# Down-phase operands requested in the last up unit, norm squares summed in PSUM, low parts on GpSimd, three more buffers

## The chip, the cores and the metric

The kernel runs on one core of a Trainium2 chip. The core has TensorE (matrix products into PSUM), VectorE (DVE in the profile), ScalarE (ACT), GpSimd (POOL) and SyncE (SP), which issues nearly all DMA transfers here. Every engine has a queue of its own that it works off in order, and engines wait for each other by semaphores. The metric is the device time in microseconds (us) of one execution.

## What is computed

One layer of a decoder trunk for a prompt of 2048 tokens and a sample group of 8 times 4 tokens, 2080 tokens in all, with 1024 channels, in 32-bit floating point. Attention in a window of 128 and a state-space block run side by side, are normalised, and go through an output projection; then comes a gated feed-forward network (FFN) with a short convolution:

```python
merged = jnp.concatenate([_rmsnorm(attn, p['g_attn']), _rmsnorm(ssm, p['g_ssm'])], axis=-1)
x = x + merged @ p['w_out']
f, conv_new = _conv_ffn(_rmsnorm(x, p['norm_ffn']), conv_prev,
                        p['w_up'], p['conv_w'], p['conv_b'], p['w_down'])
x = x + f

def _conv_ffn(h, prev, w_up, conv_w, conv_b, w_down):
    L = h.shape[1]
    up = h @ w_up
    buf = jnp.concatenate([prev.astype(up.dtype), up], axis=1)
    c = conv_b + sum(conv_w[i] * buf[:, i:i + L] for i in range(CONV_W))
    a, g = jnp.split(c, 2, axis=-1)
    return (jax.nn.silu(g) * a) @ w_down, buf[:, -(CONV_W - 1):]
```

with `_rmsnorm(x, g)` = x · rsqrt(mean(x²) + 1e-5) · g, and one more such norm at the very end.

## The kernel before

**Precision.** Every matrix product is made of three. An operand is split into a high part (a rounding to fp32r) and a low part (the rest); `mm3` adds high·high, high·low and low·high in one PSUM bank. `split` makes the two parts: line 83 casts the high part, usually on ScalarE, and line 84 subtracts it for the low part, on VectorE or GpSimd as its last argument says.

**Channels lie on the 128 partitions, tokens in the free dimension.** The work comes in stages: projections, attention and state space, then the output projection, then the FFN in two groups of tokens (`gi` 0 and 1), each with an up phase and a down phase.

**Output projection.** `TILES3` are eight tiles of 260 tokens, loop variable `it`. For each, eight output blocks `m` are computed (eight times three matmuls each, tiles `wo`), in a ring of four PSUM banks. The input block `xm` is loaded (line 1171), the product is added (line 1176) and the sum is stored to `x2scr` (line 1177). `xm` has twelve buffers. At the end of a tile `sumsq` forms the sum of squares of the eight blocks: ScalarE squares a block, VectorE adds it to `ss` in SBUF (line 133). The norm itself is computed inside the next tile, after block 1: `ffn_norm` calls `rstd_psum`, which sums over partitions with a matmul against ones (line 115), takes logarithm and exponential on ScalarE and one Newton step on VectorE (lines 119 to 121), all in the PSUM bank; eight VectorE instructions (line 1143) then scale the blocks, and each is stored to `h2scr` (line 1144). The pool `pst` has two banks for this. The last tile's norm is computed in `finish_front`, within the first up unit; only behind it are the pool of `xm` and `pst` closed, whose places go to the pool `hb` (operand q0) and to the two banks `psv` of the up phase.

**The up phase** has 21 units `j` for each `gi`. A unit uses Winograd-like sums so that seven products replace eight; the operands x0, t2, q1 and q0, each as high and low parts, are made once per phase. For `gi` 0 they come from sums stored during the output projection: `begin_ffn` loads and splits t2, `load_q(1)` q1, and `load_q(0)`, called from `finish_front`, q0. `load_wup` prepares a unit's weights (on GpSimd the low parts and four sums, lines 1265 to 1269). A unit takes eight tiles from the ring `c2`, which has ten buffers (`CB`): two `ca`, two `cb`, two `cc0`, two `cc1`. The results, high and low part, leave from the `cc` tiles to `actscr` (line 1331). `unit` takes two hooks: `begin` runs after its second product, `mid` between the two halves of its fourth.

**The down phase** runs over token tiles (two of 512 for `gi` 0; 448, 352 and 256 for `gi` 1), each with 21 operand blocks `i` and eight output blocks `m`, that is 24 matmuls for an operand block (tiles `dn`). `load_a` loads the block's high and low part (`ah`, `al`) from `actscr` into two `c2` buffers, for up to three blocks ahead (line 1464); `load_wd` loads and splits the weights (`wdr`, line 1437). In the first tile the output blocks 2, 3, 6 and 7 of the first two operand blocks are put off until the third (`ULATE` = 2), because their banks are those that the last up unit used last: blocks 0 to 3 use the pool of `ux`, 4 and 5 that of `u` (tag u2), 6 and 7 `psv`.

Instructions are put in order at build time: each engine's queue is filled by priority (the order of the code, moved forward where `tc.high_priority` says so) among what is ready, and tiles get their buffers then.

Of the kernel before, what the change touches and what calls it, by code (L numbers as in the profile page):

```python
# [18 lines left out]
P = 128  # L19
# [43 lines left out]
HPD = 90  # L63
# [46 lines left out]

def rstd_psum(c, pool, ps, ss, n, ones, nm):

    nc = c.nc
    ps = ps[:, :n]
    nc.tensor.matmul(ps, ones, ss, start=True, stop=True)
    r0 = pool.tile([P, n], F32, tag="r0", name=f"r0_{nm}")
    nc.scalar.activation(r0, ps, AF.Ln, bias=c.eps)
    nc.scalar.activation(r0, r0, AF.Exp, scale=-0.5)
    nc.vector.scalar_tensor_tensor(ps, ps, EPS, r0, ALU.add, ALU.mult)
    nc.vector.scalar_tensor_tensor(ps, ps, -0.5, r0, ALU.mult, ALU.mult)  # L120
    nc.vector.scalar_tensor_tensor(ps, ps, 1.5, r0, ALU.add, ALU.mult)
    return ps


def sumsq(c, pool, xs, n, nm, eng=None):

    nc = c.nc
    ss = pool.tile([P, n], F32, tag="ss", name=f"ss_{nm}", bufs=2)
    nc.scalar.activation(ss, xs[0], AF.Square)
    for k, x in enumerate(xs[1:]):  # L130
        sq = pool.tile([P, n], F32, tag="sq", name=f"sq_{nm}_{k}", bufs=3)
        nc.scalar.activation(sq, x, AF.Square)
        (eng or nc.vector).tensor_tensor(ss, ss, sq, ALU.add)
    return ss

# [503 lines left out]
def body(tc, a):  # L639
# [16 lines left out]
    with ExitStack() as top:  # L656
# [473 lines left out]
        with after_preload():  # L1130
# [7 lines left out]
            def ffn_norm(it, xs, ss):  # L1138
                t0, n = TILES3[it]
                r = rstd_psum(c, p3b, pst.tile([P, 512], F32, tag="st", name=f"st_f_{it}"), ss, n, ones[1024], f"f_{it}")  # L1140
                for k in range(KD):
                    h = xs[k]
                    nc.vector.scalar_tensor_tensor(h, xs[k], g_ffn[:, k : k + 1], r, ALU.mult, ALU.mult)
                    nc.sync.dma_start(h2scr[:, k, t0 : t0 + n], h)

            def begin_ffn():

                p3m_close()
                stg_close()
                st.p3e_close()  # L1150
                ffn.sp, ffn.sp_close = pool("fsp", "right")
                ffn.up, ffn.up_close = pool("fup", "right", 2)
                ffn.c2, ffn.c2_close = pool("fc2", "right", CB)
                ffn.hc, ffn.hc_close = pool("fhc", "right")
                for sub in range(2):
                    t2 = ffn.t2[sub] = hi_lo(ffn.hc, [4, W], f"t2{sub}", 0)
                    for k in range(0, 4, 2):
                        s = ffn.c2.tile([P, 2, W], F32, tag="c2", name=f"t2r_{sub}_{k}")
                        nc.sync.dma_start(s, t2scr[:, sub, k : k + 2])
                        split(nc, *[t[:, k : k + 2] for t in t2], s, nc.scalar, nc.vector)  # L1160

            old = None
            for it, (t0, n) in enumerate(TILES3):
# [5 lines left out]
                for m in range(KD):  # L1169
                    xm = p3b.tile([P, n], F32, tag="xm", name=f"xm_{it}_{m}", bufs=12)  # L1170
                    nc.sync.dma_start(xm, xTv[:, m, t0 : t0 + n])
# [17 lines left out]
                if it == len(TILES3) - 2:  # L1189
                    begin_ffn()  # L1190
                old = (it, xs, sumsq(c, p3b, xs, n, f"f_{it}", nc.vector))
        ps_close()
# [85 lines left out]
        def load_q(i):  # L1278
            for sub in range(2):
                q = (ffn.q0, ffn.q1)[i][sub] = hi_lo((hb, hd)[i], [2, 4, W], f"q{i}{sub}", 0)  # L1280
                for k in range(4):
                    s = c2.tile([P, 2, W], F32, tag="c2", name=f"q{i}r_{sub}_{k}")
                    nc.sync.dma_start(s, qscr[:, sub, i, k])
                    with tc.high_priority(offset=HPD):
                        split(nc, *[t[:, :, k] for t in q], s, nc.scalar, nc.vector if i else (nc.gpsimd, nc.vector)[k % 2])

# [145 lines left out]
        def load_wd(gi, j, t0):  # L1432
# [17 lines left out]
            return w  # L1450

        def down(gi, beside):

            old = None
            for ti, (t0, n) in enumerate(TILESD[gi]):
# [4 lines left out]

                def load_a(j):
                    hl = [dt([P, n], F32R, f"a{i}_{t0}_{j}") for i in "hl"]
                    for i, t in enumerate(hl):
                        ffn.last_sp = nc.sync.dma_start(t.bitcast(F32), actscr[:, j, 1 - i, t0 : t0 + n]).ins
                    return hl

                def one(i, m):
# [4 lines left out]

                hls = {}
                for i, j in enumerate(order):
                    for ahead in range(i, min(i + 3, NF)):
                        if ahead not in hls:
                            hls[ahead] = load_a(order[ahead])
                    ahl[i] = hls[i], load_wd(gi, j, t0)
# [28 lines left out]
        def prepare(gi):  # L1507
# [3 lines left out]
            for f in (load_sums, load_last):  # L1511
                for sub in range(2):
                    yield from f(gi, sub)

        def last_norm():
            next(last, None)

        for gi in range(2):
            for j in range(NF):
                if (gi, j) != (0, 0):  # L1520
                    ws = load_wup(gi, j)
                unit(gi, j, ws, None if j or gi else finish_front, last_norm if gi and j == 0 else None)
            beside = prepare(1) if gi == 0 else iter(())
# [128 lines left out]
```

## Time and profile before

| what | us |
|---|---|
| device time, median of 3 runs | 2220.59 |
| lowest and highest of these | 2218.52, 2222.08 |
| the profiled execution | 2218.95 |
| its span, first to last instruction | 2217.2 |
| TensorE busy in the span | 2055.2 (93%) |
| VectorE, ScalarE, GpSimd busy | 1323.1, 1054.1, 1200.4 |
| last wo matmul to first up matmul | 765.68 to 771.17 |
| first up phase's end to the first down matmul | 1217.25 to 1227.38 |
| second up phase's end to the first down matmul | 1927.09 to 1943.62 |

The profile is one execution. A row of its timeline gives the start (us from the span's start), the duration, the engine, the line of the kernel, the operation, the tiles written and read, their shape and how many instructions are merged in the row; behind it in brackets stands the idle time of that engine just before, with the instruction that ended it. SPq is SyncE's queue, where DMA transfers are issued. A wait view sums such idle time by who waited for whom. A window view gives each engine's busy time in a stretch, the clock granted to TensorE (1.00 is full) and the share of the DMA engines.

### The profile page before, as it was taken

To read this page: it belongs to the slowest core of one execution; us is meant where nothing else is said; L and a number is where in the kernel's file an instruction comes from. 1 tells how busy PE (TensorE), PEld (TensorE's weight loads), DVE (VectorE), ACT (ScalarE), POOL (GpSimd) and SP (SyncE) were. 2 spreads that over 40 slices of the span, in tenths; PEclk is the share of its full clock that TensorE was granted. 3 is DMA by queue.
4 is the path that set the end of the run, shared out by engine and by line. 5 is a ranking of instruction groups with operands and counts; after the bars stand their busy time and mean duration, and the time that the engine had idled before them with its cause. 6 is when DMAs were issued, how large, how long until landed. Compare 5 with 4: busy or idle time off the path is not lost.

```text
span 2217.2 us, 41459 instructions
## 1 busy us (share of the span) xinstructions
PE 2055.2 (93%) x14685; PEld 1926.3 (87%) x14685; DVE 1323.1 (60%) x3310; ACT 1054.1 (48%) x2459; POOL 1200.4 (54%) x1184
## 2 busy tenths in 40 slices
PE   8969999978998889999999898999999999799997
PEld 8957878857998889999999686789999999788997
DVE  8859898358566766766666165227766666601231
ACT  6525564675443356666666233225655665602111
POOL 4857776334455466666665453446666666822211
PEclk9979999989999999999999899999999999999999
DMA  7865434686478733333333795834323333573643
GB/s 230 255 149 157 123 107 130 128 232 189 147 236 255 236 125 117 108 96 110 108 107 102 248 284 177 292 130 152 112 93 110 106 101 102 175 191 118 206 131 98
DMA packets 294352, 347.59 MB, mean 157 GB/s; under 512 B 42344, under 2 KB 250864, under 8 KB 294128
## 3 DMA queue, kind: packets, MB, share of 16 engines
q1 hardware_dynamic: 294144, 344.94, 51.5%
q8 instruction: 116, 1.90, 0.4%
q14 instruction: 92, 0.75, 0.1%
HBM read 232.70 MB, written 107.80 MB: 154 GB/s over the span
## 4 chain that ended last, share of the span: by engine, by line
PE 70%; DVE 10%; DMA 7%; POOL 4%; issue 4%; ACT 3%; SPq 2%; DVEq 0%; POOLq 0%; ACTq 0%
PE ux L1345 20%; PE u L1345 16%; PE dn L90 7%; PE dn L91 7%; PE dn L89 6%; DVE xo L1427 1%; PE wo L90 1%; PE wo L91 1%; PE wo L89 1%; PE qkv L89 1%; DMA y<-yscr 1%; PE qkv L91 1%; PE qkv L90 1%; DMA al<-actscr 1%; SPq L787 1%
## 5 line engine op out<-in xcount | busy, mean ns | idle before, releaser
L84 POOL TENSOR_TENSOR wdl<-wdr,wdh 128x1024 fp32r<-128x1024 f32 x65 | 159.0, 2451 | 301.9 <-ACT wdh L83 295.2
L89 PE MATMUL dn<-ah,wdh 128*128 128x512 f32 (+3 forms) x552 | 205.7, 373 | 17.1 <-DMA ah<-actscr 14.1
L91 PE MATMUL dn<-ah,wdl 128*128 128x512 f32 (+3 forms) x552 | 205.8, 373 | 3.3 <-POOL wdl L84 3.3
L90 PE MATMUL dn<-al,wdh 128*128 128x512 f32 (+3 forms) x552 | 205.5, 372 | 1.8 <-DMA al<-actscr 1.7
L1310 ACT ACTIVATE cc<-u,cw 128x260 f32<-128x260 f32 (+1 forms) x252 | 141.5, 563 | 95.1 <-DVE u L1388 67.0
L83 ACT CAST wdh<-wdr 128x1024 fp32r<-128x1024 f32 x65 | 68.0, 1050 | 243.8 <-PE dn L90 210.6
L1502 DVE TENSOR_TENSOR xo<-xo,dn 128x512 f32<-128x512 f32 (+3 forms) x40 | 21.9, 584 | 269.7 <-PE dn L91 269.6
L84 POOL TENSOR_TENSOR wls<-s,whs 128x1024 fp32r<-128x1024 f32 x42 | 101.2, 2409 | 133.9 <-ACT whs L83 133.8
L1311 DVE SCALAR_TENSOR_TENSOR cc<-u,cw,cc 128x260 f32<-128x260 f32 (+1 forms) x252 | 120.8, 480 | 67.8 <-ACT cc L1310 66.2
L89 PE MATMUL wo<-mh,wo 128*128 128x260 f32 x512 | 149.8, 293 | 2.9 <-ACT mh L83 2.0
L90 PE MATMUL wo<-ml,wo 128*128 128x260 f32 x512 | 147.8, 289 | 3.7 <-POOL ml L84 3.6
L91 PE MATMUL wo<-mh,wo 128*128 128x260 f32 x512 | 147.1, 287 | 0.0
L89 PEld LDWEIGHTS dn<-ah,wdh 128*128 128x128 f32 x552 | 105.6, 191 | 35.4 <-DMA ah<-actscr 10.3
L1388 DVE TENSOR_TENSOR u<-u,cb 128x262 f32<-128x262 f32 x84 | 36.4, 434 | 157.3 <-PE u L1345 157.3
L89 PE MATMUL qkv<-hh_p,wqh 128*128 128x256 f32 (+1 forms) x384 | 114.7, 299 | 13.6 <-DVE vs L890 8.5
L91 PEld LDWEIGHTS dn<-ah,wdl 128*128 128x128 f32 x552 | 105.5, 191 | 20.9 <-POOL wdl L84 4.2
L90 PEld LDWEIGHTS dn<-al,wdh 128*128 128x128 f32 x552 | 105.4, 191 | 19.8 <-DMA al<-actscr 2.9
L84 POOL TENSOR_TENSOR wlt<-s,wht 128x512 fp32r<-128x512 f32 x42 | 54.2, 1289 | 122.5 <-ACT wht L83 58.0
L1312 DVE SCALAR_TENSOR_TENSOR cc<-u,cw,cc 128x260 f32<-128x260 f32 (+1 forms) x252 | 119.2, 474 | 0.8
L84 POOL TENSOR_TENSOR wlg<-wur,whg 128x1024 fp32r<-128x1024 f32 x42 | 101.6, 2419 | 28.1 <-ACT whg L83 28.1
L89 PE MATMUL dn<-ah,wd 128*128 128x448 f32 (+2 forms) x288 | 95.0, 330 | 23.0 <-DMA ah<-actscr 19.3
L90 PE MATMUL qkv<-hl_p,wqh 128*128 128x256 f32 (+1 forms) x384 | 111.1, 289 | 0.0
(569 smaller groups left out, 8351.1 us busy)
## 6 DMA issues: line engine op xcount, KB each, us to landing
actscr<-cc SPq DMA_DIRECT2D x168, 260.0 KB, 4.7
wur<-in_w_up SPq DMA_DIRECT2D x84, 512.0 KB, 4.6
wdr<-in_w_down SPq DMA_DIRECT2D x77, 512.0 KB, 4.7
x<-in_xT SPq DMA_DIRECT2D x56, 256.0 KB, 4.3
hs<-h2scr SPq DMA_DIRECT2D x44, 262.0 KB, 4.9
ah<-actscr SPq DMA_DIRECT2D x42, 256.0 KB, 3.9
al<-actscr SPq DMA_DIRECT2D x42, 256.0 KB, 4.4
mt<-mscr SPq DMA_DIRECT2D x16, 520.0 KB, 5.4
```

What stands on the lines that cost most here:

```text
L83: i = nc.scalar.copy(hi, src) if hi_eng is nc.scalar else hi_eng.tensor_copy(hi, src)
L84: return i.ins, lo_eng.tensor_tensor(lo, src, hi.bitcast(F32), ALU.subtract).ins
L89: nc.tensor.matmul(ps, w[0], x[0], start=first, stop=False)
L90: nc.tensor.matmul(ps, w[0], x[1], start=False, stop=False)
L91: nc.tensor.matmul(ps, w[1], x[0], start=False, stop=last)
L787: nc.sync.dma_start(uscr[8 * m + g].rearrange("(s h) c -> h s c", h=16), uperm[m][16 * g : 16 * g + 16])
L1310: nc.scalar.activation(cp, pp[:, 2:], AF.Identity, bias=w[3], scale=w[2])
L1311: nc.vector.scalar_tensor_tensor(cp, pp[:, 1 : npr + 1], w[1], cp, ALU.mult, ALU.add)
L1312: nc.vector.scalar_tensor_tensor(cp, pp[:, 0:npr], w[0], cp, ALU.mult, ALU.add)
L1345: nc.tensor.matmul(pt[:, :W], x[p][:, k], y[q][:, k], start=start and k + i == 0, stop=k == 3 and i == 2, skip_group_check=True)
L1388: v.tensor_tensor(c21[s], c21[s], cb[s][:, 0], ALU.add)
L1427: nc.vector.scalar_tensor_tensor(x, x, g_fin[:, k : k + 1], r, ALU.mult, ALU.mult)
```

## The change

Five edits, all in or before the FFN:

- `load_a` becomes a function beside `down`, and a new hook `load_ahead` calls it for the first two operand blocks of the down phase's first tile. It runs as `mid` of the last up unit of each phase; `down` finds the loaded tiles in `ffn.first`.
- `sumsq_psum` takes the place of `sumsq` for the FFN norm: ScalarE writes the first square into a bank of `pst`, VectorE adds the others there, and ScalarE copies the result to SBUF.
- For the last tile `rstd_psum` writes its factor to a `c2` tile in SBUF (`out`) instead of to its bank.
- The low parts of t2 and, without raised priority, of q1 are formed on GpSimd instead of VectorE.
- `xm` has fifteen buffers instead of twelve.

```diff
-def rstd_psum(c, pool, ps, ss, n, ones, nm):
+def rstd_psum(c, pool, ps, ss, n, ones, nm, out=None):
...
-    nc.vector.scalar_tensor_tensor(ps, ps, EPS, r0, ALU.add, ALU.mult)
-    nc.vector.scalar_tensor_tensor(ps, ps, -0.5, r0, ALU.mult, ALU.mult)
-    nc.vector.scalar_tensor_tensor(ps, ps, 1.5, r0, ALU.add, ALU.mult)
-    return ps
+    r = ps if out is None else out
+    nc.vector.scalar_tensor_tensor(r, ps, EPS, r0, ALU.add, ALU.mult)
+    nc.vector.scalar_tensor_tensor(r, r, -0.5, r0, ALU.mult, ALU.mult)
+    nc.vector.scalar_tensor_tensor(r, r, 1.5, r0, ALU.add, ALU.mult)
+    return r
...
+def sumsq_psum(c, pool, ps, xs, n, nm):
+
+    nc = c.nc
+    ps = ps[:, :n]
+    nc.scalar.activation(ps, xs[0], AF.Square)
+    for k, x in enumerate(xs[1:]):
+        sq = pool.tile([P, n], F32, tag="sq", name=f"sq_{nm}_{k}", bufs=3)
+        nc.scalar.activation(sq, x, AF.Square)
+        nc.vector.tensor_tensor(ps, ps, sq, ALU.add)
+    ss = pool.tile([P, n], F32, tag="ss", name=f"ss_{nm}", bufs=2)
+    nc.scalar.copy(ss, ps)
     return ss
...
             def ffn_norm(it, xs, ss):
                 t0, n = TILES3[it]
-                r = rstd_psum(c, p3b, pst.tile([P, 512], F32, tag="st", name=f"st_f_{it}"), ss, n, ones[1024], f"f_{it}")
+                out = ffn.c2.tile([P, 2, W], F32, tag="c2", name="r_f")[:, 0, :n] if it == len(TILES3) - 1 else None
+                r = rstd_psum(c, p3b, pst.tile([P, 512], F32, tag="st", name=f"st_f_{it}"), ss, n, ones[1024], f"f_{it}", out)
...
-                        split(nc, *[t[:, k : k + 2] for t in t2], s, nc.scalar, nc.vector)
+                        split(nc, *[t[:, k : k + 2] for t in t2], s, nc.scalar, nc.gpsimd)
...
-                    xm = p3b.tile([P, n], F32, tag="xm", name=f"xm_{it}_{m}", bufs=12)
+                    xm = p3b.tile([P, n], F32, tag="xm", name=f"xm_{it}_{m}", bufs=15)
...
-                old = (it, xs, sumsq(c, p3b, xs, n, f"f_{it}", nc.vector))
+                bank = pst.tile([P, 512], F32, tag="st", name=f"ssp_f_{it}")
+                old = (it, xs, sumsq_psum(c, p3b, bank, xs, n, f"f_{it}"))
...
-                    with tc.high_priority(offset=HPD):
-                        split(nc, *[t[:, :, k] for t in q], s, nc.scalar, nc.vector if i else (nc.gpsimd, nc.vector)[k % 2])
+                    with nullcontext() if i else tc.high_priority(offset=HPD):
+                        split(nc, *[t[:, :, k] for t in q], s, nc.scalar, nc.gpsimd if i else (nc.gpsimd, nc.vector)[k % 2])
...
+        def load_a(j, t0, n):
+            hl = [dt([P, n], F32R, f"a{i}_{t0}_{j}") for i in "hl"]
+            for i, t in enumerate(hl):
+                ffn.last_sp = nc.sync.dma_start(t.bitcast(F32), actscr[:, j, 1 - i, t0 : t0 + n]).ins
+            return hl
+
         def down(gi, beside):
...
-                hls = {}
+                hls = {} if ti else ffn.first
                 for i, j in enumerate(order):
                     for ahead in range(i, min(i + 3, NF)):
                         if ahead not in hls:
-                            hls[ahead] = load_a(order[ahead])
+                            hls[ahead] = load_a(order[ahead], t0, n)
...
+        def load_ahead():
+
+            for f in range(2):
+                ffn.first[f] = load_a(f, *TILESD[gi][0])
+
...
         for gi in range(2):
+            ffn.first = {}
             for j in range(NF):
                 if (gi, j) != (0, 0):
                     ws = load_wup(gi, j)
-                unit(gi, j, ws, None if j or gi else finish_front, last_norm if gi and j == 0 else None)
+                unit(gi, j, ws, None if j or gi else finish_front, (last_norm if gi else None) if j == 0 else load_ahead if j == NF - 1 else None)
```

More of the change, by code (lines that the diff above doesn't have):

```diff
@@ L133, in sumsq @@
         (eng or nc.vector).tensor_tensor(ss, ss, sq, ALU.add)
+    return ss
+def sumsq_psum(c, pool, ps, xs, n, nm):
[8 more added lines that the diff above has]
+    nc.scalar.copy(ss, ps)
     return ss
@@ L1459, in down @@
                     order = [f for i in range(7) for f in (2 * i, 2 * i + 1, 14 + i)]
[L1461 to L1465, printed above, removed]
                 def one(i, m):
```

## The prediction

> **What bounds the kernel now.** I read the page first: its span and its chain of work.
>
> ```profile
> span 2217.2 us, 41459 instructions
> ...
> PE 70%; DVE 10%; DMA 7%; POOL 4%; issue 4%; ACT 3%; SPq 2%; DVEq 0%; POOLq 0%; ACTq 0%
> ```
>
> TensorE carries the chain, so time is to be won only where TensorE stands still or runs slowly. The second view, who waited for whom, lists TensorE's waits in three stretches: the first down phase (1200 to 1245), the second (1900 to 1950) and the way from the output projection into the FFN (740 to 810). Columns: total us, times, longest.
>
> ```profile
> PE dn L89 <- DMA ah<-actscr: 10.1, 1, 10.1
> PE dn L90 <- DMA al<-actscr: 1.4, 1, 1.4
> ...
> PE dn L89 <- DMA ah<-actscr: 16.5, 1, 16.5
> ...
> PE u L1345 <- DVE xm L1143: 7.2, 1, 7.2
> PE ux L1345 <- DVE xm L1176: 5.5, 1, 5.5
> ```
>
> These are the places that the edits touch. Each is priced by asking which wait ends last once the present one is gone.
>
> **Part 1a, first operands early, first down phase.** Rows of the timeline by engine, the page's DMA issues, and windows (us, busy with count for PE, PEld, DVE, ACT, POOL, then granted clock, DMA share, GB/s):
>
> ```profile
> 1216.97 0.28 PE L1345 MATMUL ux<-q01h,wlt 128*128 128x262 f32 x1
> ...
> 1243.22 0.40 PE L89 MATMUL dn<-ah,wdh 128*128 128x512 f32 x1
> ...
> 1200.71 5.92 SPq L1331 DMA_DIRECT2D actscr<-cc  x4
> ...
> actscr<-cc SPq DMA_DIRECT2D x168, 260.0 KB, 4.7
> ...
> 1220.35 0.43 DVE L1330 TENSOR_TENSOR cc<-u,cc 128x260 fp32r<-128x260 f32 x1 [0.24 <-ACT cc L1329]
> ...
> 1225.56 0.43 DVE L1330 TENSOR_TENSOR cc<-ux,cc 128x260 fp32r<-128x260 f32 x1 [0.44 <-ACT cc L1329]
> ...
> 1227.40:1235.50 8.10, 6.69 (x15) 4.93 (x16) 0.00 (x0) 0.00 (x0) 0.00 (x0) 0.51 1.03 358
> 1235.50:1243.20 7.70, 7.70 (x34) 6.20 (x34) 0.70 (x1) 2.21 (x3) 1.60 (x1) 1.00 0.30 95
> ```
>
> The up phase's last matmul ends at 1217.25. The 48 products of the first two operand blocks are done at 1243.22. Four loads (two blocks, high and low part) move up into the last unit. The ring c2 has ten buffers; a unit takes eight, in the order ca, cb, cc0, cc1. At the new place six of the last unit's eight are taken, so the four loads get the buffers of the unit before it, whose four actscr writes are issued from 1200.71 to 1206.6 and land 4.7 later: the loads leave between about 1205 and 1211. Behind them on SP stand a small o_tail write and wdr loads for later weights, whose readers come after 1217. The last unit's cc1 pair then takes ca's buffers, read out long before. So the operands are there at 1217.25.
>
> The next wait is the PSUM banks. Blocks 0 and 1 have free banks, 4 and 5 wait for the last unit's u, released by DVE up to 1220.78; 2 and 3 are put off until after operand 1 and wait for ux, released up to 1225.99. A block is three matmuls of 0.23 (7.70 us for 34), 0.7 us. In TensorE's order: two blocks until 1218.7, block 5 until 1221.5, four blocks of operand 1 until 1224.3, block 3 from 1226.0 to 1226.7, and six blocks until 1230.9. Against 1243.22 that is 12.3 less at full clock. TensorE still stands about 2.5 us in short pieces; the present start runs at clock 0.51 for 8.1 us with 15 matmuls, which costs 3 to 4 us. If half clock comes here too, 9 remain. I take 11 (9 to 12.3).
>
> ```profile
> 687.50:692.40 4.90, 4.88 (x22) 4.88 (x23) 1.74 (x4) 1.54 (x5) 1.90 (x3) 0.50 1.01 339
> ...
> PE wo L89 <- ACT mh L83: 2.0, 2, 1.4
> PE wo L90 <- POOL ml L84: 1.3, 3, 0.5
> ```
>
> Here the clock was 0.50 for 4.9 us after five waits of 3.3 us together, none over 1.4 (between 670 and 695): short pieces can halve it. The Trainium skill, TensorE: Matmul & The Clock Gate, "What's actually happening", has the clock fall only after an idle window of about 3.4 us; by that the first phase would win 12.3 and the sum below would be 1.3 better. The trace decides, and it does not agree.
>
> **Part 1b, second down phase.** The same views:
>
> ```profile
> 1926.81 0.28 PE L1345 MATMUL ux<-q01h,wlt 128*128 128x262 f32 x1
> ...
> 1956.37 0.37 PE L89 MATMUL dn<-ah,wd 128*128 128x448 f32 x1
> ...
> 1914.17 0.36 SPq L1331 DMA_DIRECT2D actscr<-cc  x1
> 1916.29 19.05 SPq L1437 DMA_DIRECT2D wdr<-in_w_down  x9
> ...
> 1937.72 0.56 SPq L1464 DMA_DIRECT2D ah<-actscr  x1
> ...
> 1933.76 0.43 DVE L1330 TENSOR_TENSOR cc<-u,cc 128x260 fp32r<-128x260 f32 x1 [0.17 <-ACT cc L1329]
> ...
> 1944.42 0.43 DVE L1330 TENSOR_TENSOR cc<-ux,cc 128x260 fp32r<-128x260 f32 x1 [2.98 <-ACT cc L1329]
> ...
> 1943.07 1.04 ACT L83 CAST wdh<-wdr 128x1024 fp32r<-128x1024 f32 x1 [2.00 <-DMA wdr<-in_w_down]
> ```
>
> Now the loads stand behind nine wdr loads, which SP issues as GpSimd frees their buffers. Moved, they wait for the actscr write of 1914.17 to land (about 1919); the wdr loads behind them slip by up to 3 us, which GpSimd's queue of splits covers, and if it doesn't, ScalarE's casts slip as much. But the banks come late here: ScalarE's wdr casts stand between the unit's last activations, so blocks 4 and 5 open until 1934.2 and block 3 at 1944.85. TensorE does seven blocks of 0.6 by 1938.6, waits, and has seven left: 1944.85 plus 4.3, plus 1.5 for half clock, is 1950.7; 5.7 less than 1956.37. The cast at 1943.07 waited for a wdr load that today shares the DMA engines with the four moved ones, so it may come 2 us earlier: I take 6.5 (4 to 9).
>
> **Part 2, the way into the FFN.** The other edits: the squares' sums in PSUM, eight ScalarE copies, t2's and q1's low parts on GpSimd, fifteen xm buffers, the last norm's factor r in SBUF. Groups between 540 and 800, then timeline rows:
>
> ```profile
> L133 DVE TENSOR_TENSOR ss_f<-ss_f,sq_f 128x260 f32<-128x260 f32 x56 | 35.1, 627 | 31.8 <-ACT sq_f L132 29.1 <-ACT sq_m L132 2.4
> ...
> L1176 DVE TENSOR_TENSOR xm<-xm,wo 128x260 f32<-128x260 f32 x64 | 26.6, 418 | 24.3 <-DMA xm<-in_xT 12.3 <-PE wo L91 11.5
> ...
> 765.04 1.89 SPq L1171 DMA_DIRECT2D xm<-in_xT  x4
> ...
> 771.17 0.56 PE L1345 MATMUL ux<-x00h,whv 128*128 128x262 f32 x1 [5.49 <-DVE xm L1176]
> ...
> 780.25 0.38 ACT L1359 COPY ca<-ux 128x262 f32<-128x262 f32 x1 [5.22 <-POOL prev L1298]
> ...
> 784.80 0.44 DVE L119 SCALAR_TENSOR_TENSOR st_f<-st_f,r_f 128x260 f32<-128x260 f32 x1
> ...
> 786.22 3.26 DVE L1143 SCALAR_TENSOR_TENSOR xm<-xm,vec,st_f 128x260 f32<-128x260 f32 x8
> ...
> 791.05 2.22 ACT L83 CAST q00h<-q0r 128x524 fp32r<-128x524 f32 x4 [6.02 <-DMA h2scr<-xm]
> ...
> 800.85 0.39 PE L1345 MATMUL u<-q01l,whg 128*128 128x262 f32 x1 [0.41 <-POOL q01l L84]
> ...
> 774.84 2.14 POOL L1295 TENSOR_TENSOR prevt<-prev,cw 128x336 f32<-128x336 f32 x1 [17.13 <-DVE q11l L84]
> ...
> 786.39 1.27 POOL L1267 TENSOR_TENSOR s<-wur,s 128x512 f32<-128x512 f32 x1
> ...
> 795.13 1.22 POOL L84 TENSOR_TENSOR q01l<-q0r,q01h 128x524 fp32r<-128x524 f32 x1
> ...
> 1374.85 13.94 DVE L1427 SCALAR_TENSOR_TENSOR xo<-xo,vec,rs_fo 128x512 f32<-128x512 f32 x8
> ...
> 1375.36 8.09 POOL L84 TENSOR_TENSOR wdl<-wdr,wdh 128x1024 fp32r<-128x1024 f32 x3 [22.04 <-ACT wdh L83]
> ```
>
> The sums: 56 adds at about L1176's 418 ns instead of 627 give VectorE 11.7 us, of which the path sees 1 to 3, since VectorE mostly waits; the eight copies, 0.38 each by the copy at 780.25, wait on ScalarE for VectorE's last add, with the next tile's squares queued behind them; the next tile's blocks on TensorE cover that, uncovered it is 3.0. The sums' bank was emptied by the copy a tile before, so no wait is added there. I take 1.5. Twelve low parts cost GpSimd 1.22 each: t2's four are covered by the idle 17.1 us before 774.84, uncovered 4.9. The loss of the raised priority I cost at nothing: ScalarE's casts of q1 have no rival for their place, and at 0.55 each (791.05) a swap is worth less than that.
>
> The waits of 5.5 and 7.2: with fifteen buffers only the last xm load, not four, follows the norm of the tile before, so the first up matmul can start 5 us sooner; and with r in SBUF the bank is free after L119, 4.2 us before L1143's end. Together up to 9.2. But the same unit also needs q0. Its buffers lie where xm was, so the casts at 791.05 wait for h2scr, that is for L1143, and the product at 800.85 follows L1143's end (789.48) by 11.4. What counts is when L1143 ends. Its start can move from 784.8 to about 776 (5 for the sooner start, the rest from ScalarE's wait at 780.25). With r in SBUF, however, ten operations (two of r's and the eight) read two SBUF operands, and at 1374.85 eight of that kind took 1.74 each beside GpSimd splits of 2.70 (three in 8.09), while L1143's eight, whose factor is in PSUM today, take 0.41 each. GpSimd is now full there: eight low parts of q1 (9.8 us; they lie where the projection's weights were, so from about 766.5) and the 12.8 us that now run from 774.84 to 787.66. Ten operations, each let in after one GpSimd instruction of about 1.1 and with 0.4 of its own, end at 776 + 15 = 791, about as now. So this stage wins nothing, perhaps loses 0.5. The ends: 9 won if GpSimd is out of the way, 6.5 lost if L119 stays at 784.8 and its followers alternate with GpSimd. I take 0.5 lost.
>
> The Trainium skill, SBUF — State Buffer, "Who interferes with whom", calls this an exclusive lock between a VectorE instruction with two SBUF inputs and a GpSimd one that reads SBUF, held for the whole instruction; it speaks for the sums in PSUM and against r in SBUF, and 1374.85 agrees.
>
> **The sum.** 11 + 6.5 + 1.5 - 0.5 = 18.5 us. The profiled execution took 2218.95 us (span 2217.2, 1.75 around it), so 2200.5; it is 1.6 below the median 2220.59, and as a median I forecast 2202.
>
> **The rivals.**
> - GpSimd does not hold up VectorE (for it: VectorE also waits for ScalarE, and GpSimd could idle; against: the price at 1374.85). The FFN starts 9 sooner: 2193.
> - The banks decide more than I allow: the second down phase wins nothing, since the casts slip, and the FFN starts 3 later: 11 + 1.5 - 3 = 9.5, 2211. For it: 1943.07; against: GpSimd's queue covers 3 us.
> - The change doesn't do what it says: the loads still issue behind the wdr loads (1937.72). Then 1 remains: 2219.5.
> - Slower: the loads hold SP. If their buffers are not the earlier unit's but cb's of the last one, which come free near 1933 to 1936, SP stands from about 1916 until then, the nine wdr loads start up to 19 us later, GpSimd's splits and ScalarE's casts about 14 later, and block 3's bank opens near 1959: 1964.8 against 1956.37, 8.4 lost; with nothing won in the first phase and 1 in part 2, 2228. It decides once SP stands beyond about 1930. Against it: the ring's order above.
>
> **How the numbers follow.** Forecast 0.50 (2196 to 2208), GpSimd aside 0.15, banks 0.17, no effect 0.08, slower 0.10. The range 2190 to 2214 holds the first three, 0.82, and all the bounds of part 1. A measurement of this kernel tells 0.2%, 4.4 us, from no change: faster 0.82, same 0.08, slower 0.10.
>
> **What would show it.** Right: ah and al of the first two blocks issue before 1212 and 1920; TensorE's first dn matmul comes within 1 us of the last up matmul; its next waits name DVE; L1143 takes about 1.5 us each in the last norm. Wrong: SP standing at these loads; a wait for GpSimd in the units after the first; the halved clock gone or longer.

## The result, and the profile after

| | kernel before | changed kernel |
|---|---|---|
| median of four runs, us | 2221.34 | 2196.52 |
| lowest and highest | 2218.52, 2230.71 | 2189.93, 2199.05 |
| the profiled execution | 2218.95 | 2194.39 |

The ratio is 0.9873 (95% interval 0.9852 to 0.9894): 1.3% faster. Two executions in a slow state, one of run 10 (5214 us) and one of the kernel before beside runs 1 to 4 (2851 us), are left out of all medians, ranges and ratios below. The time lies in the forecast range (2190 to 2214), 5.5 us below the forecast of 2202. From profile to profile the gain is 24.6 us where the sum said 18.5.

The page of the changed kernel gives its span and the chain of work that ended last, still TensorE's, with 75% of it where 70% were:

```profile
span 2192.2 us, 41498 instructions
...
PE 75%; DVE 8%; DMA 6%; issue 4%; ACT 3%; POOL 3%; SPq 2%; DVEq 0%; ACTq 0%; POOLq 0%
```

The next view is that of who waited for whom, for TensorE, in the three stretches that the prediction read (740 to 810, 1200 to 1245, 1900 to 1950; us in total, times, longest):

```profile
PE u L1362 <- ACT q00h L83: 9.3, 1, 9.3
PE u L1362 <- POOL q00l L84: 2.4, 1, 2.4
PE u L1362 <- DVE r_f L120: 1.9, 1, 1.9
PE ux L1362 <- DVE xm L1192: 0.6, 1, 0.6
PE u L1362 <- DVE cc L1347: 0.6, 1, 0.6
...
PE dn L89 <- DVE cc L1347: 1.5, 3, 0.8
...
PE dn L89 <- DVE cc L1347: 5.8, 3, 2.8
```

Both waits for `ah` are gone (10.1 and 16.5), and what is late next in both down phases is the banks that VectorE releases, as forecast. In the first stretch the waits of 5.5 and 7.2 have become 0.6 and 1.9, but one of 9.3 has come for q0. (Lines moved: 1345 is now 1362, 1330 is 1347, 1143 is 1159, 1176 is 1192, 119 to 121 are 120 to 122.)

The timeline of the changed kernel shows the loads and the joints of the phases:

```profile
1197.21 0.46 SPq L1472 DMA_DIRECT2D ah<-actscr  x1
...
1209.84 0.29 PE L1362 MATMUL ux<-q01h,wlt 128*128 128x262 f32 x1
1209.96 0.40 PE L89 MATMUL dn<-ah,wdh 128*128 128x512 f32 x1
...
1223.72 0.39 PE L89 MATMUL dn<-ah,wdh 128*128 128x512 f32 x1
...
1895.22 0.38 SPq L1472 DMA_DIRECT2D ah<-actscr  x1
...
1908.93 0.28 PE L1362 MATMUL ux<-q01h,wlt 128*128 128x262 f32 x1
1909.05 0.37 PE L89 MATMUL dn<-ah,wd 128*128 128x448 f32 x1
...
1929.78 0.36 PE L89 MATMUL dn<-ah,wd 128*128 128x448 f32 x1
```

The first of the four early loads is shown for each phase. They issue 8 to 13 us ahead of the first phase's end, 1210.13 (forecast 6 to 12), and 11 to 14 ahead of the second's, 1909.21 (forecast about 8), and the first down matmul follows the last up matmul without a gap. The 49th down matmul (the first behind the 48 of two operand blocks) starts at 1223.72 and 1929.78. With it the span can be cut into stretches, each from rows of TensorE's timeline, and the gain be laid beside the terms of the forecast:

| stretch, us | before | after | gain | forecast |
|---|---|---|---|---|
| up to the first `wo` matmul | 549.3 | 547.4 | 1.9 | none |
| first to last `wo` matmul | 216.4 | 211.7 | 4.7 | 1.5 |
| from there to unit 1 of the up phase | 39.0 | 38.9 | 0.1 | -0.5 |
| rest of the first up phase | 412.6 | 412.2 | 0.4 | none |
| its end to the 49th down matmul | 26.0 | 13.6 | 12.4 | 11 |
| to the end of the second up phase | 683.9 | 685.5 | -1.6 | none |
| its end to the 49th down matmul | 29.3 | 20.6 | 8.7 | 6.5 |
| to the last matmul | 251.8 | 253.4 | -1.6 | none |

The gains add up to 25.0. Nothing was changed ahead of the first `wo` matmul, so its 1.9 us is chance; among all the runs below this point lay between 546.1 and 549.7.

The last stretch of the FFN's way in is that of the last norm. The timeline of VectorE and, beside it, GpSimd:

```profile
770.55 0.43 DVE L120 SCALAR_TENSOR_TENSOR r_f<-st_f,r_f 128x260 f32<-128x260 f32 x1 [1.33 <-ACT r_f L118]
771.01 4.39 DVE L121 SCALAR_TENSOR_TENSOR r_f<-r_f,r_f 128x260 f32<-128x260 f32 x1
775.44 1.41 DVE L122 SCALAR_TENSOR_TENSOR r_f<-r_f,r_f 128x260 f32<-128x260 f32 x1
776.88 8.27 DVE L1159 SCALAR_TENSOR_TENSOR xm<-xm,vec,r_f 128x260 f32<-128x260 f32 x8
...
769.16 4.71 POOL L84 TENSOR_TENSOR q11l<-q1r,q11h 128x524 fp32r<-128x524 f32 x4
773.83 1.29 POOL L84 TENSOR_TENSOR wlt<-s,wht 128x512 fp32r<-128x512 f32 x1
```

L120 starts at 770.55 where the forecast had 776; counted from the last `wo` matmul that is 11.5 us, against 19.1 before. From there to the end of L1159 (785.15) it takes 14.6 us, against 4.7 before (784.80 to 789.48); the forecast had 15. L121 alone stood until the last of the four `q11l` instructions and the one behind them were done. Of the eight of L1159, the four beside GpSimd's next instructions took 1.38 to 2.56 us, the four behind these 0.47.

### The profile page after: what moved, and what is told of

Its sections match the earlier page's. It is cut to its first block, busy times and chain, and to the rows that moved or that the text cites. A ratio compares the mean times of both kernels' runs of the same rounds, so it can differ in the third digit from the quotient of the medians.

```text
span 2192.2 us, 41498 instructions
## 1 busy us (share of the span) xinstructions
PE 2054.4 (94%) x14685; PEld 1923.5 (88%) x14685; DVE 1307.6 (60%) x3298; ACT 1055.8 (48%) x2467; POOL 1208.9 (55%) x1196
## 4 chain that ended last, share of the span: by engine, by line
PE 75%; DVE 8%; DMA 6%; issue 4%; ACT 3%; POOL 3%; SPq 2%; DVEq 0%; ACTq 0%; POOLq 0%
PE ux L1362 21%; PE u L1362 16%; PE dn L90 6%; PE dn L89 6%; PE dn L91 6%; PE wo L90 2%; PE wo L91 2%; PE wo L89 2%; PE qkv L89 2%; PE qkv L91 1%; PE qkv L90 1%; DVE xo L1444 1%; SPq L802 1%; PE u L91 1%; DMA mt<-mscr 1%
## 5 line engine op out<-in xcount | busy, mean ns | idle before, releaser
L520 POOL TENSOR_SCALAR s_b<-s_b,den_b 128x256 f32<-128x256 f32 x128 | 75.4, 605 | 63.2 <-DVE den_b L518 38.4
```

The source lines that it names most:

```text
L520: nc.gpsimd.tensor_scalar(s[:, h], s[:, h], den[:, h : h + 1], 1.0, ALU.mult, ALU.mult)
```

## The experiments

Twelve kernels, each timed in five rounds beside the kernel before on the same chip. "From first `wo`" is the time from the first `wo` matmul to unit 1, of which the `wo` stretch and unit 0 (first up matmul to unit 1) are parts; "49th" are the two stretches from an up phase's end.

| run | median (lowest to highest) | ratio to before (95%) | `wo` | unit 0 | from first `wo` | 49th, first and second |
|---|---|---|---|---|---|---|
| kernel before | 2221.3 (2218.5 to 2230.7) | 1 | 216.4 | 33.5 | 255.4 | 26.0, 29.3 |
| changed kernel | 2196.5 (2189.9 to 2199.1) | 0.9873 (0.9852 to 0.9894) | 211.7 | 38.2 | 250.5 | 13.6, 20.6 |
| 1 early loads alone | 2204.3 (2203.1 to 2207.0) | 0.9925 (0.991 to 0.994) | 220.8 | 33.4 | 259.7 | 13.8, 21.2 |
| 2 no early loads | 2212.3 (2209.3 to 2215.1) | 0.9958 (0.9944 to 0.9973) | 210.2 | 38.4 | 249.1 | 23.7, 29.3 |
| 3 twelve `xm` | 2198.8 (2196.7 to 2203.2) | 0.9903 (0.9884 to 0.9921) | 216.9 | 41.6 | 259.6 | 13.6, 20.5 |
| 4 q1 on VectorE | 2190.7 (2190.3 to 2193.7) | 0.9864 (0.9848 to 0.9881) | 209.9 | 35.4 | 245.9 | 13.6, 20.7 |
| 5 r in PSUM | 2188.5 (2184.6 to 2190.7) | 0.9845 (0.9821 to 0.9869) | 211.8 | 35.8 | 248.2 | 13.6, 21.2 |
| 6 both 4 and 5 | 2191.7 (2182.8 to 2192.6) | 0.9853 (0.9829 to 0.9877) | 209.4 | 34.4 | 244.4 | 13.6, 21.2 |
| 7 casts later | 2185.8 (2184.8 to 2186.7) | 0.9835 (0.9813 to 0.9857) | 212.4 | 37.2 | 250.3 | 13.6, 11.7 |
| 8 banks in turn | 2188.8 (2187.1 to 2194.8) | 0.9854 (0.9831 to 0.9876) | 209.1 | 37.7 | 247.3 | 11.4, 15.9 |
| 9 sums in SBUF | 2203.7 (2201.3 to 2209.0) | 0.9917 (0.9899 to 0.9935) | 216.6 | 39.4 | 258.0 | 13.8, 20.7 |
| 10 fifteen `xm` alone | 2219.2 (2207.6 to 2223.8) | 0.9989 (0.9972 to 1.0005) | 219.9 | 33.2 | 255.8 | 22.8, 30.0 |
| 11 three together | 2176.4 (2170.5 to 2177.4) | 0.9791 (0.977 to 0.9813) | 211.1 | 36.8 | 248.5 | 11.4, 9.6 |
| 12 t2 on VectorE | 2190.4 (2188.7 to 2196.1) | 0.9862 (0.9839 to 0.9885) | 210.7 | 39.8 | 251.1 | 13.6, 20.3 |

Two medians 4 us apart can't be told from each other here; the stretches are one execution each, and the same code in them varied by 4.5 us in the `wo` stretch (216.4 and 220.8 in the kernel before and run 1, whose instructions there are the same) and by about 1 us in unit 0.

**The two halves of the change (runs 1 and 2).** Run 1 adds the early loads alone to the kernel before, run 2 takes them alone from the changed kernel:

```diff
-unit(..., (last_norm if gi else None) if j == 0 else load_ahead if j == NF - 1 else None)
+unit(..., (last_norm if gi else None) if j == 0 else None)
```

> The kernel before with the early loads of the down phases' first operands alone. Theory (the parts add up): between the two profiles the 49th matmul of the first down phase came 12.4 us sooner against the end of the up phase, that of the second 8.7 us, and some 3 us were given back later in the down phases; alone the loads bring 18 to 21 us, 2200 to 2203 where the kernel before takes 2221, and the FFN's start stays within 1 us of the kernel before. Rival (the loads gain so much only because the FFN starts sooner, with emptier queues): 12 us or less, 2209 or more, with waits of over 3 us or a halved clock back in the first down phase.

> The changed kernel without the early loads; the four edits ahead of the FFN stay. Theory: the 7.1 us by which unit 0 of the up phase ended sooner are kept to the end, 2213 to 2216 where the kernel before takes 2221, and the waits of 10 and 16 us for ah come back. Rival (as forecast: these edits are worth 1 us): 2219 to 2222, the gain being lost at a later wait.

Run 1 is 17.8 us faster than the kernel before (2222.1 beside it), run 2 9.8. The waits of TensorE in run 1, in the first and the second down phase:

```profile
PE dn L89 <- DVE cc L1330: 1.8, 3, 1.1
...
PE dn L89 <- DVE cc L1330: 6.9, 4, 3.6
```

The two halves add up to 27.6, about the 24.8 of the whole. So the loads gain what they gain without the rest: the rival of run 1 falls, and the time lies 1 us beyond the theory's 2200 to 2203. Its FFN started 3.0 us later than in the kernel before (774.17 against 771.17), not within 1, since the same `wo` instructions took 4.5 us longer there. In run 2 the waits for `ah` are back (10.3 and 16.3 us), and its time lies 1 us below the theory's 2213 to 2216. Its rival, the forecast's own value of 1 us for the other edits, falls: they are worth 6 to 12 (interval of the ratio, 0.27% to 0.56%).

**The projection (runs 3, 9, 10).** What shortened it, the buffers or the sums?

```diff
# run 3
-xm = p3b.tile([P, n], F32, tag="xm", name=f"xm_{it}_{m}", bufs=15)
+xm = p3b.tile([P, n], F32, tag="xm", name=f"xm_{it}_{m}", bufs=12)
# run 9
-old = (it, xs, sumsq_psum(c, p3b, bank, xs, n, f"f_{it}"))
+old = (it, xs, sumsq(c, p3b, xs, n, f"f_{it}", nc.vector))
# run 10, on the kernel before
-xm = ... bufs=12)
+xm = ... bufs=15)
```

> The changed kernel with twelve xm buffers again, nothing else undone. Theory (the buffers carry the sooner end of the projection): VectorE waits for the xm loads again, 8 us or more in 560 to 770, TensorE's first up matmul waits 4 to 6 us for it as before, and L122 and L1159 of the last norm start as much later: 3 to 6 us longer than the changed kernel, 2200 to 2203. Rival (the sums in PSUM carry it): within 1.5 us of the changed kernel, 2195 to 2198.

> The changed kernel with the squares summed in SBUF again. Theory (the sums are worth little, since VectorE waits for ScalarE's squares anyway): within 3 us of the changed kernel, 2195 to 2200; from the first output-projection matmul to the last 210 to 214 us (211.7 in the changed kernel's profile, 216.4 in that of the kernel before). Rival (the sums carry the shorter projection): 215 us or more there, and 2200 to 2204.

> The kernel before with fifteen xm buffers, nothing else. Theory (the buffers alone take away VectorE's waits for the xm loads, 12.3 us in 560 to 770, and the first up matmul's wait): the wait of 5.5 us falls below 1.5, unit 0 ends 4 to 8 us sooner after the first output-projection matmul than the 255 us of the kernel before, 2213 to 2217 where the kernel before takes 2221. Rival (the last norm still waits for q1's low parts and for the squares, so nothing is won): within 2 us of the kernel before.

VectorE's groups between 545 and 770 (busy us, mean ns, idle us before and what ended it), first the changed kernel, then run 3, then run 9:

```profile
L1192 DVE TENSOR_TENSOR xm<-xm,wo 128x260 f32<-128x260 f32 x64 | 26.8, 421 | 29.2 <-PE wo L91 28.9 <-DMA h2scr<-xm 0.2
...
L146 DVE TENSOR_TENSOR ssp_f<-ssp_f,sq_f 128x260 f32<-128x260 f32 x56 | 24.2, 432 | 38.7 <-ACT sq_f L145 38.6
```

```profile
L1192 DVE TENSOR_TENSOR xm<-xm,wo 128x260 f32<-128x260 f32 x64 | 26.9, 420 | 39.8 <-PE wo L91 20.1 <-DMA xm<-in_xT 19.4
```

```profile
L134 DVE TENSOR_TENSOR ss_f<-ss_f,sq_f 128x260 f32<-128x260 f32 x56 | 34.7, 620 | 37.7 <-ACT sq_f L133 37.6
```

TensorE's waits between 545 and 770 for the low parts of the merged operand, in the same order:

```profile
PE wo L90 <- POOL ml L84: 1.3, 3, 0.4
```

```profile
PE wo L90 <- POOL ml L84: 4.5, 6, 1.6
```

```profile
PE wo L90 <- POOL ml L84: 5.3, 9, 2.0
```

With twelve buffers VectorE stands 19.4 us for the `xm` loads; with the sums in SBUF it adds for 34.7 us instead of 24.2, 620 ns each instead of 432. Either is enough to keep the stretch long: it is 209 to 212 us in all nine kernels that have both edits and 216 to 221 in all five that lack one or both.

The buffers alone (run 10) win nothing that can be measured in time; taken from the changed kernel (run 3), they cost 2 to 7 us, the sums (run 9) 7 to 10 (the difference of the medians and of the ratios). For run 3 the intervals overlap, so there the stretch decides. So neither theory of one carrier holds: the two edits need each other. The expectation of run 9 (within 3 us) was wrong and its rival's numbers came; in run 3 VectorE's waits for the loads came back, but TensorE's first up matmul waited 1.2 us for it, not 4 to 6. In run 10 that wait fell from 5.5 to 2.7, not below 1.5, and unit 1 came no sooner after the first `wo` matmul (255.8).

How VectorE's time reaches TensorE is argued and was not followed step by step: TensorE waits 0.4 to 1.7 us for `ml` in the nine kernels and 3.5 to 5.7 in the five, and `ml` is split from what VectorE has normalised (`mf`, L1005).

**The last norm (runs 4, 5, 6, 12).** The norm now starts sooner and takes longer. Here r is the norm's factor. Run 5 puts r back in its PSUM bank, run 4 q1's low parts back on VectorE with raised priority, run 6 does both, run 12 puts t2's low parts back.

```diff
# run 5
-out = ffn.c2.tile([P, 2, W], F32, tag="c2", name="r_f")[:, 0, :n] if it == len(TILES3) - 1 else None
+out = None
# run 4
-with nullcontext() if i else tc.high_priority(offset=HPD):
-    split(nc, *[t[:, :, k] for t in q], s, nc.scalar, nc.gpsimd if i else (nc.gpsimd, nc.vector)[k % 2])
+with tc.high_priority(offset=HPD):
+    split(nc, *[t[:, :, k] for t in q], s, nc.scalar, nc.vector if i else (nc.gpsimd, nc.vector)[k % 2])
# run 12
-split(nc, *[t[:, k : k + 2] for t in t2], s, nc.scalar, nc.gpsimd)
+split(nc, *[t[:, k : k + 2] for t in t2], s, nc.scalar, nc.vector)
```

> The changed kernel with q1's eight low parts on VectorE again, with raised priority as before. Theory 1 (VectorE's queue: eight low parts of 0.32 us, 5.1 together, stand ahead of the last square's add and so of the last norm): the norm starts about 5 us later but, with GpSimd emptier, its ten operations take 4 to 9 us instead of 14.6, so the fourth product of unit 0 gets its q0 within 3 us of the changed kernel: 2194 to 2200. Theory 2 (GpSimd does not hold VectorE up; the ten take 14.6 us here too): the norm ends 5 us later and so does the kernel, 2201 to 2203. Theory 3 (the lock is all that counts): the norm ends over 3 us sooner, 2193 or less.

> The changed kernel with the last norm's factor r in its PSUM bank again; q1's low parts stay on GpSimd. Theory (two operands in SBUF make VectorE take turns with GpSimd): the ten operations take 0.4 to 0.5 us each, 4.7 to 5.5 us together instead of 14.6, though GpSimd is as busy beside them; the bank comes free 4 us later than with r in SBUF, so the fourth product waits some 4 us more for it, but q0 is there 7 to 9 us sooner: unit 0 ends 4 to 7 us sooner, 2190 to 2193. Rival (the ten are held up by something else, as the stores of h2scr or ScalarE): they take over 10 us here too, and the kernel is slower than the changed one by the 4 us of the bank, 2198 to 2202.

> Both: q1's low parts on VectorE and r in PSUM. Theory (the norm's start and its pace are two terms): it starts some 3 us later than with q1 on GpSimd, the ten operations take 4.7 us, and unit 0 ends within 2 us of the run with q1 on VectorE alone and of the one with r in PSUM alone: 2188 to 2193. Rival (the gains add up): 2186 or less.

> The changed kernel with t2's four low parts on VectorE again. Theory (GpSimd has them covered, near 742 to 748, and VectorE waits for ScalarE's squares there): within 2 us of the changed kernel, 2195 to 2199, and from the first output-projection matmul to the start of unit 1 (250.5 us in the changed kernel) 249 to 253. Rival (VectorE's last tile is tight, and every low part there puts off the last square's add as q1's did): 3 us or more slower, 2200 or more.

Run 5's timeline, VectorE and GpSimd:

```profile
770.00 0.44 DVE L120 SCALAR_TENSOR_TENSOR st_f<-st_f,r_f 128x260 f32<-128x260 f32 x1 [1.27 <-ACT r_f L118]
770.48 0.44 DVE L121 SCALAR_TENSOR_TENSOR st_f<-st_f,r_f 128x260 f32<-128x260 f32 x1
...
771.42 3.26 DVE L1159 SCALAR_TENSOR_TENSOR xm<-xm,vec,st_f 128x260 f32<-128x260 f32 x8
...
768.65 4.69 POOL L84 TENSOR_TENSOR q11l<-q1r,q11h 128x524 fp32r<-128x524 f32 x4
```

GpSimd does the same work at the same time as in the changed kernel, and only the place of r differs: L121 takes 0.44 us instead of 4.39, and the norm from L120 on 4.7 instead of 14.6. That GpSimd holds VectorE up when both its operands lie in SBUF is thus shown, and the rival of run 5 falls. But unit 0 is only 2.4 us shorter, not 4 to 7: TensorE waits 6.7 us for the bank that r in SBUF had freed early, and 3.6 for q01's low parts, the last of which now stands on GpSimd behind a split of weights (785.26, 2.35 us). The median is 8.0 us lower than the changed kernel's, with intervals of the ratios that overlap, so part of that is chance or lies where the edit does not reach.

Run 4 shows the other side:

```profile
757.76 4.49 DVE L84 TENSOR_TENSOR q10l<-q1r,q10h 128x524 fp32r<-128x524 f32 x4 [0.29 <-ACT q10h L83]
762.18 4.51 DVE L84 TENSOR_TENSOR q11l<-q1r,q11h 128x524 fp32r<-128x524 f32 x4
766.61 0.42 DVE L146 TENSOR_TENSOR ssp_f<-ssp_f,sq_f 128x260 f32<-128x260 f32 x1
...
772.09 1.49 DVE L121 SCALAR_TENSOR_TENSOR r_f<-r_f,r_f 128x260 f32<-128x260 f32 x1
...
775.05 5.42 DVE L1159 SCALAR_TENSOR_TENSOR xm<-xm,vec,r_f 128x260 f32<-128x260 f32 x8
```

The eight low parts again stand ahead of the last square's add (here for 9.0 us beside a busy GpSimd; 5.1 in the kernel before, where GpSimd stood idle for most of it, 0.64 each and not the 0.32 of the expectation), and the norm starts 14.6 us after the last `wo` matmul instead of 11.5; but with GpSimd emptier it takes 8.9 us instead of 14.6 and so, counted from that matmul, ends 2.6 sooner. So both the place in VectorE's queue and the contention count, as theory 1 of run 4 had it, and here the contention outweighs: unit 0 is 2.8 us shorter. Theory 2 falls with the 8.9. Theory 3 falls with the later start, though the time, 2190.7, lies in its range and not in that of theory 1.

In unit 0 the two undone together (34.4) win 3.8, less than the 5.2 of one by one (35.4 and 35.8 against 38.2), as run 6's theory had it, though the variation of 1 us is nearly as large as that difference. By their times, runs 4, 6 and 12 can't be told from the changed kernel. Run 12's median, 2190.4, lies below both its ranges and 6 us below the changed kernel's, but the stretch that its edit touches is not shorter (251.1 against 250.5); its profile is 3.6 us shorter, and that lies in the long stretch from the first 49th matmul up to the end of the second up phase (681.7 against 685.5), which its edit does not touch. What made it was not found.

**The banks of the second down phase (runs 7 and 8).** The 5.8 us of waits there are not all. Windows of the changed kernel (the last columns: granted clock, DMA share, GB/s), and ScalarE and VectorE in its timeline:

```profile
1910.30:1914.30 4.00, 1.00 (x4) 0.48 (x3) 2.81 (x8) 3.50 (x7) 4.00 (x2) 0.92 0.74 202
1914.30:1920.00 5.70, 5.68 (x15) 5.13 (x16) 2.19 (x6) 3.46 (x6) 5.70 (x4) 0.50 0.95 301
1920.10:1923.80 3.70, 0.94 (x4) 0.51 (x2) 2.21 (x6) 2.95 (x7) 3.70 (x2) 0.95 0.91 271
1923.80:1927.00 3.20, 3.15 (x8) 2.81 (x9) 0.00 (x0) 0.00 (x0) 2.72 (x2) 0.51 1.00 306
```

```profile
1915.54 0.38 ACT L1344 ACTIVATE ux<-cc 128x260 f32<-128x260 f32 x1
1917.88 1.05 ACT L83 CAST wd<-wdr 128x1024 fp32r<-128x1024 f32 x1 [1.96 <-DMA wdr<-in_w_down]
1918.83 0.37 ACT L1346 CAST cc<-ux 128x260 fp32r<-128x260 f32 x1
...
1919.23 0.43 DVE L1347 TENSOR_TENSOR cc<-ux,cc 128x260 fp32r<-128x260 f32 x1 [2.50 <-ACT cc L1346]
...
1923.37 0.43 DVE L1347 TENSOR_TENSOR cc<-ux,cc 128x260 fp32r<-128x260 f32 x1 [0.84 <-ACT cc L1346]
```

A cast of weights that are needed much later stands 1.96 us for its load, the last step of an activation stands behind it, and VectorE behind that. The next activation follows in the same queues, and with it the bank that TensorE waits for last: VectorE releases it at 1923.80, and TensorE goes on at 1923.85. Run 7 queues the casts of the fifth and later blocks behind the unit's last activation; run 8 leaves them and asks for the banks in the order in which they open.

```diff
# run 7
-            ffn.last_act, ffn.last_pool = split(nc, *w, r, nc.scalar, nc.gpsimd)
+            with tc.issue_after(ffn.last_cast) if gi and t0 == TILESD[1][0][0] and j >= 4 else nullcontext():
+                ffn.last_act, ffn.last_pool = split(nc, *w, r, nc.scalar, nc.gpsimd)
...
-                nc.scalar.copy(cg.bitcast(F32R), g)
+                ffn.last_cast = nc.scalar.copy(cg.bitcast(F32R), g).ins
# run 8
-                        behind, wait = (2, 3, 6, 7), ULATE
+                        behind, wait = range(KD), ULATE
...
+                                if ti == 0:
+                                    late.sort(key=lambda f: (0, 1, 5, 7, 2, 3, 4, 6)[f[1]])
                                 for li, lm in late:
```

> The changed kernel with ScalarE's casts of the second down phase's weights from the fifth block on queued behind the last unit's activations. Theory (those casts, standing for their loads ahead of the activations, make the banks late): from the second up phase's end to the 49th matmul 20.6 us become 11 to 14, as in the first phase (13.6), with no halved clock, and no wait for wd later: 6 to 9 us less than the changed kernel, 2188 to 2191. Rival 1 (VectorE's own chain sets the banks): 19 us or more, same time. Rival 2 (the casts are late then): waits for wd behind the 100th matmul eat it up, 2194 to 2198.

> The changed kernel with the first two operand blocks of each phase's first down tile multiplied output block by output block in the order 0, 1, 4, 5, 6, 2, 7, 3, both operands for a block before the next, so that TensorE asks for each late bank as late as it can with two operands. Theory (the second phase waits for banks in the wrong order): its 20.6 us to the 49th matmul become 15 to 18, the first phase's 13.6 become 12 to 13.5; 3 to 6 us less, 2190 to 2194. Rival (the last bank decides alone): the 49th matmul comes within 1.5 us of the changed kernel's.

Run 7's waits and timeline, then run 8's waits and a window:

```profile
PE dn L89 <- DVE cc L1347: 1.8, 1, 1.8
```

```profile
1915.20 0.38 ACT L1346 CAST cc<-ux 128x260 fp32r<-128x260 f32 x1 [0.41 <-DVE ux L1345]
1915.47 2.00 ACT L83 CAST wdh<-wdr 128x1024 fp32r<-128x1024 f32 x2
...
1930.33 1.05 ACT L83 CAST wd<-wdr 128x1024 fp32r<-128x1024 f32 x1 [10.95 <-DMA wdr<-in_w_down]
```

```profile
PE dn L89 <- DVE cc L1347: 4.9, 3, 2.7
```

```profile
1905.00:1930.00 25.00, 20.00 (x95) 16.86 (x94) 8.62 (x21) 11.59 (x22) 17.93 (x8) 1.00 0.91 288
```

In run 7 the last activation's last step is done at 1915.58, 6.8 us after that phase's end of the up matmuls (1908.77), against 1923.33 and 14.1 in the changed kernel. 20.6 us become 11.7, and none is lost later for the weights: theory right, both rivals fall; the time, 2185.8, is 2 us below what was expected. Run 8 wins 4.7 there and 2.2 in the first down phase (11.4, better than the expected 12 to 13.5), with the clock at 1.00: its theory is right, too. Its time, 2188.8 where 2190 to 2194 was expected, can't be told from the changed kernel's by the ratios; the stretches show the gain.

**Together (run 11).** r in PSUM, the casts later and the banks in turn:

> The changed kernel with three things that the runs point to: r of the last norm in its PSUM bank, the weight casts behind the last activations, and the late banks in turn. Theory (they lie in three different stretches: 8.0, 10.7 and 2 us, the last counted in the first down phase alone, since in the second the casts already have the banks): 2174 to 2179. Rival (part is lost where the second down phase asks for its weights, or one stretch gives back what another wins): 2182 or more.

2176.4: 20.2 us below the changed kernel, where the expectation's three gains make 20.7 (8.0 and 10.7 from the medians of runs 5 and 7, 2 from the stretch of run 8). The theory's time came, but in the profiles the stretches that the edits touch give 15.1 (2.0, 2.2 and 10.9); 5.0 lie in the long stretch between them, whose cause is open. In the second down phase (1900 to 1950) no wait of TensorE is left, and the 48 matmuls take 9.6 us. On the way into the FFN two waits stay:

```profile
PE u L1362 <- DVE xm L1159: 7.8, 1, 7.8
PE u L1362 <- POOL q01l L84: 3.6, 2, 3.0
```

## Why the prediction was right, and where its sizes were off

- **The mechanism of part 1 was right**: the loads are in place at the up phase's end, VectorE's banks are late next, SP doesn't stand at them; alone they win 17.8 where 11 + 6.5 were forecast.
- **1a, 11, measured 12.4.** The working gave 12.3 at full clock; 1.3 was taken off for a half clock after short waits, and there was none (1.00 from 1205 to 1225, waits of 1.5 us together). The forecast had listed the halved clock's being gone as a sign of its being wrong; it is gone here, and only this 1.3 hung on it.
- **1b, 6.5, measured 8.7.** The mis-sized term is the opening of block 3's bank: taken 17.8 us after the up phase's end, or 15.8 with the loads out of the way, measured 14.6 (1923.85 against 1909.21). What follows it was right: 4.3 + 1.5 forecast, 5.9 measured. The clock halves twice here, but its first stretch, 1914.3 to 1920, lies ahead of a bank that is late anyway.
- **Part 2, 1.5 - 0.5 = 1 us: the term of the projection failed.** Run 2 gives 9.8 us by time for these edits, the one profile 4.8. "The path sees 1 to 3" priced the sums by themselves, and the buffers only at the first up matmul; 1.5 was taken. But the loads and the sums both hold VectorE's tile back, and only both edits together shorten the `wo` stretch: its mean is 210.7 us in the nine kernels with both and 218.1 in the five others, 7.4 less. The profile of the kernel before, with 216.4, lies at the short end of these five, so 4.7 there is less than the term's size.
- **The way from the last `wo` matmul to unit 1, -0.5, measured 0.1: about right.** The first up matmul comes 4.9 us sooner and unit 0 takes 4.7 longer. The norm's start was near, too: 776 lies 10.3 us behind the last `wo` matmul of the kernel before, measured 11.5 behind that of the changed kernel; 770.55 is sooner because that matmul came 6.6 us sooner. What the forecast left out is that q1's eight low parts leave VectorE's queue ahead of the norm, which is worth 3.1 us of its start (run 4). That the start came out near without it is luck. T2's low parts lie at 741.7 to 749.2, not in the idle time before 774.84 that was to cover them; they cost nothing all the same (run 12).
- **The ten operations, 15 us forecast, 14.6 measured.** That GpSimd holds them up was right (run 5); that the sum came out so near was luck. The forecast let each in after one GpSimd instruction, 1.5 us for each. L121 stood through several (4.39), four of L1159 took 1.38 to 2.56, and the last four took 0.47, as GpSimd then stood waiting for q0's cast (from 783.27 to 787.85).
- **The rival of a GpSimd that holds nobody up** (2193) is wrong in its mechanism, though its time lay nearer than the forecast's 2202: the projection and the two down phases won 3.2, 1.4 and 2.2 us more than forecast in the profile, while the way into the FFN won 0.1, not 9.
- **Given back:** 1.6 us in each of two long stretches without an edit, which the sum had at nothing. The other runs have 680.5 to 688.4 and 252.4 to 256.2 there, and run 10, whose instructions there are those of the kernel before (683.9 and 251.8), 684.8 and 252.6; whether it is chance or a price of the change stays open.

## What to carry to other kernels

When an engine's chain has two bounds, a load that comes late and work that takes long, price the edits to both together: one alone may be worth nothing and the pair the whole. When work leaves an engine's queue, look for what stood behind it there, and ask of the new place with whom it takes turns. Once a wait for a load is gone, look for casts that stand for their data in the queue ahead of the steps that free PSUM banks: moving them was worth as much here as the early loads of that phase.

## What the runs showed of the hardware

- A VectorE instruction with two SBUF operands did not only wait for the GpSimd instruction that was running: L121 took 4.39 us (4.1 to 4.4 in six kernels with r in SBUF and q1 on GpSimd, 0.76 in one) while GpSimd went through instructions of 1.18 us back to back. The eight of L1159 then took 1.38 to 2.56 each beside a busy GpSimd and 0.47 beside an idle one. GpSimd pays too: its sums of 128x512 took 1.34 to 1.44 us beside L122 and L1159, 1.27 in the kernel before beside L1143, whose factor was in PSUM. The Trainium skill, SBUF — State Buffer, "Who interferes with whom", has such a pair contend for a shared read interface; run 5 agrees, and the standing through several instructions goes beyond it.
- The granted clock changed on a fixed raster: in all fourteen traces every stretch at one clock, but for the first and last, lasts a multiple of 3.41 us. In the second down phase of the changed kernel TensorE was busy for 1.08 of the 3.41 us from 1910.22 (waits of 1.45 and 1.57) and for 0.60 of those from 1920.46 (one wait of 2.81); the clock was 0.50 behind both. In run 8 a wait of 2.71 falls on two steps of the raster, each with 1.9 to 2.1 us of work, and in run 7 one of 1.80 left 1.61; the clock stayed at 1.00. So what tells these cases apart is how much of a step TensorE works, and not the longest wait. The bound is not sharp by this measure: in the kernel before the clock halved behind 2.19 us of work (from 682.38). The Trainium skill, TensorE: Matmul & The Clock Gate, "What's actually happening", asks for an idle window of about 3.4 us; none of these waits was that long, and steps with up to 2.19 us of work were idle enough. No run tried this by itself.
